# Low parts of the mixing stage's weights, made during the first feed forward and fetched from DRAM

## The chip, the core and the metric

The program runs on one core of a Trainium2 chip. The metric is the device time of one execution in microseconds (us). The core's engines each run their own instructions strictly in the program's order: TensorE (PE in the profile, PEld for its weight loads), VectorE (DVE), ScalarE (ACT), GpSimd (POOL) and SyncE (SP). SP, ACT and POOL also issue DMAs; an issue that has to wait holds up what stands behind it on that engine.

## What is computed

The reference is a chain of transformer blocks on 512 tokens of width 1024, all in float32: a dilated-window attention, a differential attention, and then a second block, cut here to what matters:

```python
x = x + 0.5 * swiglu_ffn(rms_norm(x, ffn1_norm[l]), ffn1_w_in[l], ffn1_w_out[l])   # first feed forward
h = rms_norm(x, mix_norm[l])
q_a, k_a, v_a, q_i, k_i, w_i, u_s, q_m, gates = jnp.split(h @ w_in[l], offsets, axis=-1)
o_a = indexed_sparse_attention(...) @ w_o_a[l]
y_s = jax.nn.gelu(s5_layer(u_s, ...))                 # a complex recurrence over the tokens
glu_a, glu_b = jnp.split(y_s @ w_glu[l], 2, axis=-1)
o_b = glu_a * jax.nn.sigmoid(glu_b)
o_m = memory_attention(q_m, m_k, m_v) @ w_o_m[l]
g = jax.nn.sigmoid(gates.reshape(b_, s_, N_BRANCHES, D_MODEL))
merged = g[:, :, 0] * o_a + g[:, :, 1] * o_b + g[:, :, 2] * o_m
x = x + merged @ w_out[l]                             # ends the mixing stage
x = x + 0.5 * swiglu_ffn(rms_norm(x, ffn2_norm[l]), ffn2_w_in[l], ffn2_w_out[l])
```

## The kernel before, in words

**Weights in two parts.** Each product of activations with weights is done as three matmuls in a rounded format (`mm3`, lines 153 to 155): every operand is kept as a high part and a low part, the low part being what the rounding leaves over. Activations are `uh`, `ul` (or `yh`, `yl`), weights `wh`, `wl`. Weights come in pieces of 128 partitions by 1024 columns (a few by 512 or 904). `_load` (line 300) issues a piece's DMA on SP into `raw`, of which there are two buffers. `_split` makes the two parts with `split`: ACT rounds `raw` into `wh` (line 175), DVE subtracts `wh` from `raw` into `wl` (line 176). `wh` and `wl` are rings of four buffers. A piece is split up to three pieces ahead of its use; PE needs about 5.4 us for a piece of the feed forward.

**Steps.** `tok` (tokens by output columns) and `feat` (columns by tokens) put their pieces in the list `plan` and add a step. Their sums stand in four PSUM banks, `pp`. In the first feed forward a step fills all four: PE can begin the next step only as ACT and DVE empty them (`sg`, lines 923 and 924, for the hidden units; `xa`, line 1656, for the output).

**Side work.** Coroutines (`co`) put other work between the matmuls. They wait on a clock that only the matmuls' estimated times advance; the framework then schedules what was recorded, keeps each engine's list in that order or near it, and adds the waits. `prepare` (line 1355) starts one at the beginning of the first feed forward: it normalizes the memory tokens, makes the tables of the recurrence on POOL (`s5_setup`, lines 1060 to 1069) and stores them to DRAM one by one (`s5tab<-s5cs`, line 1068), and makes the bias table (`bias_table`). The tables pass through two buffers of the pool `aux`, with the tags `memx0` and `memx1`; a tag has one buffer here.

**The mixing stage.** `mix` first projects keys, index and memory queries, then the recurrence's inputs `us` and the queries `q`, and then runs the branches: gates from `w_in`, outputs by `w_o_m` and `w_glu`. Between these matmuls stand the memory attention, the choice of keys (`score`, 16 rounds of maximum and replace), the recurrence (`s5wr`, `s5wi`) and the sparse attention. Their matmuls stand in PE's one list among those of the projections.

Of the kernel before, what the change touches and what calls it, by code (L numbers as in the profile page):

```python
# [9 lines left out]
F32 = mybir.dt.float32  # L10
FR = mybir.dt.float32r
# [8 lines left out]
P = 128  # L20
D = 1024
S = 512
# [3 lines left out]
BIG = 3.0e38  # L26
RAW, RING, AHEAD = 2, 4, 2
RQ = 2

S5GAP, SPGAP = 10.0, 2.5  # L30
KKS, KKG, HDG = 2, 8.0, 10.0
# [9 lines left out]
class Act:  # L41


    def __init__(self, n):
        self.z = [None] * n
        self.done = set()
# [19 lines left out]
class Net:  # L66
    def __init__(self, ctx, tc, consts):
        self.tc, self.nc = tc, tc.nc
        pool = lambda name, bufs, **kw: ctx.enter_context(tc.tile_pool(name=name, bufs=bufs, **kw))
        self.open = lambda c, name, bufs: c.enter_context(tc.tile_pool(name=name, bufs=bufs, reuse_waits="tile"))  # L70
        self.consts = consts
        self.cpool = pool("consts", 1)
        self.rings = {"u": pool("u", 2), "y": pool("y", 2)}
        self.wraw = pool("wraw", RAW)
        self.wsplit = pool("wsplit", RING)
        self.small = pool("small", 2)
        self.pp = pool("pp", 4, space=PSUM)
        self.pa = pool("pa", 4, space=PSUM)
        self.dram = pool("dram", 1, space=DRAM)
        self.flip = self.open_xn = 0  # L80
        self.spare_dve = False
        self.clock, self.seq, self.heap = 0.0, 0, []
        self.steps, self.plan = [], []
        self.raws, self.ready, self.live = [], {}, 0


    def at(self, delay, fn):
# [203 lines left out]
    def _load(self):  # L291
# [10 lines left out]
            o += m  # L302
        self.raws.append(raw)

    def _split(self):
        i = self.next_split
        raw = self.raws[i]
        n, nk = raw.shape[2], raw.shape[1]
        h, l = (self.wsplit.tile([P, 1024], FR, name="w" + x, tag="w" + x)[:, :nk * n]
                .rearrange("p (k c) -> p k c", k=nk) for x in "hl")  # L310
        self.split(raw, h, l)
        self.ready[i] = [(h[:, j, :], l[:, j, :]) for j in range(nk)]
        self.raws[i] = None
        self.next_split += 1
        self.live += 1
        self._load()
# [101 lines left out]
    def roped(self, x, w_in, c0, out, tmp, flags):  # L418

        nc = self.nc  # L420
        for j0 in range(0, 4, 2):
            def ev(c, ps, tok, j0=j0):
                sw = tmp().tile([P, S], F32, name="rq", tag="rq", bufs=RQ)
                for b in range(0, P, 32):
# [75 lines left out]
    def dilated(self, u, w_in, y, enter):  # L500
# [53 lines left out]
        def gate0(c, ps, _):  # L554
            sg = self.silu_gate2(v["tmp"], ps[c], "rq", RQ)
            self.need(lambda: state.get("comb0"))
            self.gated(state["f0", c], [z[:, c, :] for z in state["y0"]], y, c, sg)
# [192 lines left out]
    def differential(self, u, w_in, lams, subln, linit, y, enter):  # L750
# [53 lines left out]
        for hh in range(2):  # L804
            def ev_gate(c, ps, _, hh=hh):
                if (hh, c) in heads:
                    sg = self.silu_gate2(v["tmp"], ps[c], "rq", RQ)
                    self.gated(heads[hh, c], [z[:, c, :] for z in heads["y", hh]], y, 4 * hh + c, sg)
# [546 lines left out]
    def prepare(self, a, pre, aux):  # L1355

        nc = self.nc
        v = {}
        gc = v["gc"] = pre.tile([P, 4], F32, name="gc")
        for i, nm in enumerate(("a_q_gain", "a_k_gain", "m_q_gain", "m_k_gain")):  # L1360
            for h in range(2):
                nc.gpsimd.dma_start(gc[h * 64:h * 64 + 64, i:i + 1], a[nm].unsqueeze(1))
        v["mkT"] = pre.tile([P, 2, 256], F32, name="mkT")
        v["mv"] = pre.tile([P, 2, 256], F32, name="mv")
        v["mk"] = set()
        m = v["mem"] = Act(KT)
        m.g = [tuple(aux.tile([P, 4, 256], FR, name="mT%d%s" % (i, x)) for x in "hl") for i in range(2)]
        m.z = [(g[0][:, j, :], g[1][:, j, :]) for g in m.g for j in range(4)]
        self.mixv = v

        def gen():
            g = self.gain(aux, a["mem_norm"], "gmem")
            for t in range(2):
                xt = aux.tile([P, D], F32, name="memx%d" % t)
                nc.gpsimd.dma_start(xt, a["mem"][t * P:(t + 1) * P, :])
                yield 5.0
                self.norm_u(aux, xt, self.row_rstd(aux, xt), g, t, m)
                yield 10.0
            yield from self.s5_setup(a, pre, aux)
            yield 5.0  # L1380
            v["btab"] = self.bias_table(a["rel_bias"], a["onehot"], aux)

        self.co(gen())

    def mix(self, u, a, enter, merged):

        nc, tc = self.nc, self.tc
        V, G = nc.vector, nc.gpsimd
        w = a["w_in"]
# [32 lines left out]
        def raw(name):  # L1422
            self.need(bm.free)
            return v["at"].tile([P, S], F32, name=name, tag="bm", bufs=bm.n), bm.take()
# [30 lines left out]
        def ev_heads(key, nh, dst, col):  # L1455
            def ev(t, ps):
                def gen():
                    r, held = raw(key + "r")
                    yield from self.heads_T(r, room(), v["st"], ps, nh, v[dst], v["gc"][:, col:col + 1], t)
                    held[0] = True  # L1460
                    flags[key].add(t)
                self.run_now(gen())
            return ev
# [26 lines left out]
            self.co(gen())  # L1490

        self.tok(ux, [(w, 1220, 256)], ev_heads("qm", 4, "qmT", 2), by="t")
        self.feat(ux, [(w, 964, 256)], ev_us)
        self.add(start_s5)
        self.tok(ux, [(w, 0, 512)], ev_heads("q", 8, "qaT", 0), by="t")
# [2 lines left out]
        def branch(b, o, wo, first, last):  # L1498
            nk = len(o.z)
            if first:  # L1500
                for f in range(0, KT, 2):
                    def ev_first(c, ps, _, f=f):
                        nc.scalar.activation(v["M"][f + c], ps[c], AF.Tanh, scale=0.5)

                    self.feat(ux, [(w, 1476 + b * D + f * P, 256)], ev_first)
                for f in range(0, KT, 2):
                    def ev_prod(c, ps, _, f=f):
                        M = v["M"][f + c]
                        V.scalar_tensor_tensor(M, M, 1.0, ps[c], op0=OP.add, op1=OP.mult)

                    self.feat(lambda: o, [(wo, f * P, 256)], ev_prod, nk=nk)
                return
            for f in range(0, KT, 2):
                th = []

                def ev_gate(c, ps, _, th=th):
                    s = v["sg"].tile([P, S], F32, name="sgm", tag="sgm")
                    nc.scalar.activation(s, ps[c], AF.Tanh, scale=0.5)
                    th.append(s)

                def ev_o(c, ps, _, f=f, th=th):
                    M = v["M"][f + c]
                    V.scalar_tensor_tensor(th[c], th[c], 1.0, ps[c], op0=OP.add, op1=OP.mult)
                    G.tensor_tensor(M, M, th[c], op=OP.add)
                    if last and f == KT - 2:
                        self.at(1.5, lambda: finish(f + c))

                def ev_glu(c, ps, _, f=f, th=th):
                    if c < 2:
                        return  # L1530
                    M = v["M"][f + c - 2]
                    s = v["sg"].tile([P, S], F32, name="glt", tag="sgm")
                    nc.scalar.activation(s, ps[c], AF.Tanh, scale=0.5)
                    V.scalar_tensor_tensor(s, s, 1.0, ps[c - 2], op0=OP.add, op1=OP.mult)
                    V.scalar_tensor_tensor(s, th[c - 2], 1.0, s, op0=OP.add, op1=OP.mult)
                    V.scalar_tensor_tensor(M, s, 0.5, M, op0=OP.mult, op1=OP.add)

                self.feat(ux, [(w, 1476 + b * D + f * P, 256)], ev_gate)
                if last and f == KT - 2:
                    def most():  # L1540
                        for k in range(KT - 2):
                            self.at(1.2 * k, lambda k=k: finish(k))
                    self.add(most)
                if b == 1:
                    self.feat(lambda: o, [(wo, f * P, 256), (wo, D + f * P, 256)], ev_glu, nk=nk)
                else:
                    self.feat(lambda: o, [(wo, f * P, 256)], ev_o, nk=nk)
# [8 lines left out]
        merged.done = set(range(NT))  # L1556
        branch(2, om, a["w_o_m"], True, False)
        branch(1, ys, a["w_glu"], False, False)

        def leave():  # L1560
            self.need(lambda: v.get("a done") and v.get("s5 done"))
            v["inner"].close()
# [15 lines left out]
    def run(self, a, out):  # L1578
        nc, tc = self.nc, self.tc
# [4 lines left out]
        pool = lambda c, name, bufs=1: self.open(c, name, bufs)  # L1584
# [100 lines left out]

        def enter_mix():
            self.need(lambda: len(self.mixv["mk"]) == 2)
            s3.close()
            return s2

# [121 lines left out]
```

## Time and profile before

| | us |
|---|---|
| median of 3 runs (2160.23 to 2167.46) | 2166.17 |
| the profiled execution | 2165.69 |
| its span, first to last instruction | 2163.9 |
| outside the span | 1.8 |
| PE busy | 2103.0 (97%) |
| DVE busy | 1237.9 (57%) |

The steps here are sums on the profiled execution, which lies 0.5 us under the median. In the span the first feed forward runs from about 920 to 1305 us, the projections that open the mixing stage follow from 1330, and the stretch in which the attentions and the recurrence stand between the matmuls goes from 1390 to 1610. A row of the timeline gives the start, the time taken, engine, line, operation and tiles, and in brackets how long the engine had been idle before and what ended that.

### The profile page before, as it was taken

Reading aid. Unit: us, or ns where it says so; the run is one execution under the profiler, and the core shown is the slowest. Engines: PE = TensorE matmul, PEld = TensorE weight load, DVE = VectorE, ACT = ScalarE, POOL = GpSimd, SP = SyncE. Lnnn points to the kernel's source line nnn. Section 1 sums busy time; section 2 is a strip of 40 time slices with the busy share of each in tenths; the row PEclk is TensorE's granted clock in tenths of the full one; section 3 lists DMA queues with packets and bytes.
Section 4 is the critical chain, followed back from the end, with each engine's and each line's share of the span. In section 5 each row is a group of like instructions: output and inputs, shape, how many; then the busy total and the mean of one; then the engine's idle time right before and its main releaser. Section 6 shows DMA issues by size and latency. Waiting matters only on the chain.

```text
span 2163.9 us, 27643 instructions
## 1 busy us (share of the span) xinstructions
PE 2103.0 (97%) x10217; PEld 1709.3 (79%) x10217; DVE 1237.9 (57%) x2673; ACT 938.7 (43%) x1885; POOL 234.5 (11%) x322
## 2 busy tenths in 40 slices
PE   7999999999999999999999999988899999999998
PEld 6888988889888776788888888755567888888887
DVE  5645457454667677876543337889885454333334
ACT  4746455464545655555223234433344234223223
POOL 0000000000000000110970000124431100000000
PEclk9999999999999999999999999989999999999999
DMA  5222222212233212233343334222243323333332
GB/s 176 88 69 69 69 70 63 83 59 69 80 127 127 88 59 69 98 120 109 117 146 98 98 98 154 79 60 74 64 143 97 110 81 99 97 97 98 98 98 78
DMA packets 152055, 204.11 MB, mean 94 GB/s; under 512 B 9848, under 2 KB 111240, under 8 KB 151920
## 3 DMA queue, kind: packets, MB, share of 16 engines
q1 hardware_dynamic: 138368, 170.70, 25.8%
q10 hardware_dynamic: 8352, 15.14, 2.4%
q0 software_dynamic: 5200, 16.50, 2.1%
q8 instruction: 80, 1.31, 0.3%
q14 instruction: 55, 0.45, 0.1%
HBM read 191.80 MB, written 10.51 MB: 93 GB/s over the span
## 4 chain that ended last, share of the span: by engine, by line
PE 49%; DVE 8%; ACT 2%; DMA 1%; issue 1%; POOL 1%; ACTq 0%; DVEq 0%; POOLq 0%; SPq 0%
PE pp L153 15%; PE pp L154 15%; PE pp L155 15%; PE pa L159 3%; PE pa L164 1%; DVE wl L176 1%; DVE s5wi L1148 1%; DVE score L1262 1%; DVE s5wr L1147 1%; DMA raw<-in_w_in 1%; ACT wh L175 1%; DVE s5t L1150 0%; ACT p L438 0%; DVE m L1261 0%; POOL s5wr L1142 0%
## 5 line engine op out<-in xcount | busy, mean ns | idle before, releaser
L176 DVE TENSOR_TENSOR wl<-raw,wh 128x1024 fp32r<-128x1024 f32 (+1 forms) x320 | 410.4, 1283 | 496.1 <-ACT wh L175 494.9
L175 ACT CAST wh<-raw 128x1024 fp32r<-128x1024 f32 (+1 forms) x320 | 333.7, 1044 | 636.8 <-PE pp L154 287.5
L153 PE MATMUL pp<-uh,wh 128*128 128x512 f32 (+1 forms) x1232 | 485.0, 394 | 0.2 <-DVE sg L445 0.2
L154 PE MATMUL pp<-ul,wh 128*128 128x512 f32 (+1 forms) x1232 | 478.2, 388 | 1.0 <-DVE ul L282 1.0
L155 PE MATMUL pp<-uh,wl 128*128 128x512 f32 (+1 forms) x1232 | 477.5, 388 | 0.0
L153 PEld LDWEIGHTS pp<-uh,wh 128*128 128x128 f32 x1232 | 232.0, 189 | 54.4 <-issue 9.9
L155 PEld LDWEIGHTS pp<-uh,wl 128*128 128x128 f32 x1232 | 232.4, 189 | 46.0 <-issue 0.6
L154 PEld LDWEIGHTS pp<-ul,wh 128*128 128x128 f32 x1232 | 233.0, 189 | 43.7 <-DVE ul L282 1.2
L153 PE MATMUL pp<-wh,uh 128*128 128x512 f32 (+2 forms) x592 | 237.9, 403 | 0.3 <-ACT wh L175 0.2
L154 PE MATMUL pp<-wl,uh 128*128 128x512 f32 (+2 forms) x592 | 229.2, 388 | 0.5 <-DVE wl L176 0.4
L155 PE MATMUL pp<-wh,ul 128*128 128x512 f32 (+2 forms) x592 | 228.6, 387 | 0.0
L153 PE MATMUL pp<-yh,wh 128*128 128x512 f32 (+1 forms) x464 | 176.0, 379 | 0.0
L154 PE MATMUL pp<-yl,wh 128*128 128x512 f32 (+1 forms) x464 | 175.1, 377 | 0.0
L155 PE MATMUL pp<-yh,wl 128*128 128x512 f32 (+1 forms) x464 | 174.8, 377 | 0.0
L425 ACT COPY rq<-pp 32x512 f32<-32x512 f32 x256 | 148.0, 578 | 58.0 <-PE pp L155 52.8
L153 PEld LDWEIGHTS pp<-wh,uh 128*128 128x128 f32 x592 | 127.8, 216 | 21.2 <-issue 4.6
L154 PEld LDWEIGHTS pp<-wl,uh 128*128 128x128 f32 x592 | 128.3, 217 | 17.3 <-DVE wl L176 1.8
L155 PEld LDWEIGHTS pp<-wh,ul 128*128 128x128 f32 x592 | 127.6, 215 | 16.6 <-issue 0.3
L153 PE MATMUL pp<-wh,yh 128*128 128x512 f32 x304 | 119.2, 392 | 0.1
L154 PE MATMUL pp<-wl,yh 128*128 128x512 f32 x304 | 118.8, 391 | 0.0
L155 PE MATMUL pp<-wh,yl 128*128 128x512 f32 x304 | 118.6, 390 | 0.0
L438 ACT ACTIVATE sm<-sm,nm 128x128 f32<-128x128 f32 (+1 forms) x192 | 79.8, 417 | 54.4 <-DVE nm L437 54.1
(404 smaller groups left out, 2774.4 us busy)
## 6 DMA issues: line engine op xcount, KB each, us to landing
raw<-in_ffn_w_in SPq DMA_DIRECT2D x176, 256.0 KB, 3.1
raw<-in_dil_w_in SPq DMA_DIRECT2D x80, 512.0 KB, 3.6
raw<-in_ffn_w_out SPq DMA_DIRECT2D x44, 512.0 KB, 3.7
raw<-in_diff_w_in SPq DMA_DIRECT2D x32, 512.0 KB, 3.7
raw<-in_w_in SPq DMA_DIRECT2D x32, 512.0 KB, 3.7
raw<-in_dil_w_out SPq DMA_DIRECT2D x8, 512.0 KB, 3.7
raw<-in_diff_w_out SPq DMA_DIRECT2D x8, 512.0 KB, 3.6
s5tab<-s5cs POOLq DMA_DIRECT2D x8, 512.0 KB, 3.3
```

The lines of the kernel that those rows point to most:

```text
L153: mm(ps, a[0], b[0], start=first, stop=False)
L154: mm(ps, a[0], b[1], start=False, stop=False)
L155: mm(ps, a[1], b[0], start=False, stop=last)
L159: self.nc.tensor.matmul(ps, a, b, start=start, stop=stop)
L164: self.nc.tensor.transpose(ps, x, self.ident[:n, :n])
L175: self.nc.scalar.copy(h, src)
L176: return self.nc.vector.tensor_tensor(l, src, h.bitcast(F32), op=OP.subtract)
L425: nc.scalar.copy(sw[b:b + 32, :], ps[c][b ^ 32:(b ^ 32) + 32, :])
L438: nc.scalar.activation(sm, sm, AF.Exp, bias=nm, scale=-1.0, accum_out=den)
L1147: V.tensor_tensor_scan(wr, mag, wr, 0.0, op0=OP.mult, op1=OP.add)
L1148: V.tensor_tensor_scan(wi, mag, wi, 0.0, op0=OP.mult, op1=OP.add)
L1262: V.match_replace(sc[:, :n], m8, sc[:, :n], -BIG)
```

## The change

A new coroutine, `low_parts`, runs at the end of `prepare`'s side work, so in the second half of the first feed forward. `self.early` names the pieces of the mixing stage from `us` to the end of the second branch, 30 of them; the loop ends when the mixing stage opens (`early_on`), and gets 25 done. For each piece it loads the weights on POOL's queue into a buffer `wr0` (with the tag `memx0`), lets ACT round them into `wh0` (tag `memx1`), lets DVE subtract in place, and stores the result to DRAM as `low`, again on POOL's queue. Between these halves the coroutine waits 4 us of the estimated clock (`EGAP`). In the mixing stage a piece that has a stored low part is still loaded as before and rounded on ACT, but its `wl` is fetched from DRAM by a DMA on SP; the subtract on DVE is gone.

```diff
+    def low_parts(self, pool):
+        nc = self.nc
+        for i in range(*self.early):
+            yield EGAP
+            if not self.early_on:
+                return
+            parts, k0, nk = self.plan[i]
+            n = sum(p[2] for p in parts)
+            r, h = (pool.tile([P, 2, S], F32, name=nm, tag=tag).rearrange("p a b -> p (a b)")[:, :nk * n].rearrange(
+                "p (k c) -> p k c", k=nk) for nm, tag in (("wr0", "memx0"), ("wh0", "memx1")))
+            o = 0
+            for w, c0, m in parts:
+                nc.gpsimd.dma_start(r[:, :, o:o + m],
+                                    w[k0 * P:(k0 + nk) * P, c0:c0 + m].rearrange("(k p) c -> p k c", p=P))
+                o += m
+            yield EGAP
+            if not self.early_on:
+                return
+            self.split(r, h.bitcast(FR), r.bitcast(FR))
+            low = self.dram.tile([P, nk, n], F32, name="low")
+            nc.gpsimd.dma_start(low, r)
+            self.low[i] = low
...
-        self.split(raw, h, l)
+        if i in self.low:
+            self.nc.scalar.copy(h, raw)
+            self.nc.sync.dma_start(l.bitcast(F32), self.low.pop(i))
+        else:
+            self.split(raw, h, l)
...
             v["btab"] = self.bias_table(a["rel_bias"], a["onehot"], aux)
+            yield from self.low_parts(aux)
...
         def enter_mix():
             self.need(lambda: len(self.mixv["mk"]) == 2)
+            self.early_on = False
             s3.close()
             return s2
```

Line numbers after the change are larger by 2 at `split` and by 30 from the steps on. On DVE, in the first feed forward just behind the copies of the bias table (`brow`), the list was:

```order
L176 TENSOR_TENSOR wl<-raw,wh 128x1024 x3
L1656 SCALAR_TENSOR_TENSOR xa_7835<-pp,xa_7835 128x512
L1656 SCALAR_TENSOR_TENSOR xa_7836<-pp,xa_7836 128x512
L1656 SCALAR_TENSOR_TENSOR xa_7837<-pp,xa_7837 128x512
L1656 SCALAR_TENSOR_TENSOR xa_7838<-pp,xa_7838 128x512
L176 TENSOR_TENSOR wl<-raw,wh 128x1024 x4
L924 TENSOR_TENSOR sg<-sg,pp 128x512 x2
```

The same place on DVE after the change:

```order
L178 TENSOR_TENSOR wl<-raw,wh 128x1024 x2
L178 TENSOR_TENSOR wr_9418<-wr_9418,wh_9419 128x1024
L178 TENSOR_TENSOR wl<-raw,wh 128x1024
L1690 SCALAR_TENSOR_TENSOR xa_7835<-pp,xa_7835 128x512
L1690 SCALAR_TENSOR_TENSOR xa_7836<-pp,xa_7836 128x512
L1690 SCALAR_TENSOR_TENSOR xa_7837<-pp,xa_7837 128x512
L1690 SCALAR_TENSOR_TENSOR xa_7838<-pp,xa_7838 128x512
L178 TENSOR_TENSOR wr_9487<-wr_9487,wh_9488 128x1024
L178 TENSOR_TENSOR wl<-raw,wh 128x1024 x2
L178 TENSOR_TENSOR wr_9564<-wr_9564,wh_9565 128x1024
```

The first subtract of an early piece stands before the third `wl` and the four `xa`, which empty the `pp` banks; ACT's list has the matching rounding of `wr` at the same place, between two roundings of `raw`.

On POOL, the end of the tables of the recurrence was followed only by the stores of `xa` at the end of the feed forward:

```order
L1188 DMA btab<-brow 8x640
L1065 TENSOR_TENSOR s5cs<-e_8867,e_8868 128x512 x2
L1067 TENSOR_TENSOR s5cs<-s5cs,s5t 128x512 x2
L1068 DMA s5tab<-s5cs 128x1024
L1668 DMA x_82<-xa_7835 128x1024
```

After the change the early pieces stand there, a load and a store in turn:

```order
L1218 DMA btab<-brow 8x640
L1095 TENSOR_TENSOR s5cs<-e_8867,e_8868 128x512 x2
L1097 TENSOR_TENSOR s5cs<-s5cs,s5t 128x512 x2
L1098 DMA s5tab<-s5cs 128x1024
L320 DMA wr_9418<-in_w_in 128x4x256
L328 DMA low<-wr_9418 128x1024
L320 DMA wr_9487<-in_w_in 128x4x256
L328 DMA low<-wr_9487 128x1024
```

No load of an early piece moved ahead of the tables; each load of `wr` waits for the store before it, since they use one buffer.

On SP, the DMA list of the mixing stage's gates and `w_o_m` was:

```order
L300 DMA raw<-in_w_in 128x2x512 x4
L300 DMA raw<-in_w_in 128x4x256 x8
L300 DMA raw<-in_w_o_m 128x2x256 x4
L300 DMA raw<-in_w_in 128x4x256 x2
L300 DMA raw<-in_w_glu 128x2x256 x2
```

After the change, at the change from the gates to `w_o_m`:

```order
L302 DMA raw<-in_w_in 128x4x256
L339 DMA wl<-low 128x1024
L302 DMA raw<-in_w_o_m 128x2x256
L339 DMA wl<-low 128x1024
L302 DMA raw<-in_w_o_m 128x2x256
L339 DMA wl<-low 128x512
```

The fetch of a low part stands between the loads of `raw`, one for each piece.

## Rows read from the trace of the kernel before

**Rows 1.** Page, part 1: busy us (share of the span) and instructions.
```profile
PE 2103.0 (97%) x10217; PEld 1709.3 (79%) x10217; DVE 1237.9 (57%) x2673; ACT 938.7 (43%) x1885; POOL 234.5 (11%) x322
```

**Rows 2.** Stretches A:B: length, busy PE, PEld, DVE, ACT, POOL, PE clock, DMA.
```profile
1131.00:1300.00 169.00, 169.00 (x747) 139.96 (x746) 58.08 (x63) 46.09 (x55) 0.00 (x0) 1.00 0.32 97
1392.00:1608.00 216.00, 184.63 (x784) 123.09 (x784) 192.50 (x399) 79.37 (x195) 86.80 (x80) 0.94 0.28 80
1400.00:1420.00 20.00, 16.41 (x63) 10.82 (x62) 16.45 (x44) 6.66 (x17) 6.04 (x7) 0.83 0.08 27
```

**Rows 3.** Whom PE waited for, 1340 to 1680: us, times, longest.
```profile
PE pa L164 <- ACT msm L438: 11.6, 8, 2.2
...
PE pa L164 <- DVE anm L437: 4.3, 1, 4.3
...
PE pp L153 <- ACT wh L175: 0.2, 1, 0.2
```

**Rows 4.** Stretch 1360:1610, instructions on `wl` alone: PE, PEld, DVE.
```profile
1360.00:1610.00 250.00, 74.32 (x190) 37.02 (x190) 31.11 (x26) 0.95 0.30 86
```

**Rows 5.** Timeline of DVE: first and last subtract in the stretch with PE's idle time.
```profile
1435.16 1.22 DVE L176 TENSOR_TENSOR wl<-raw,wh 128x1024 fp32r<-128x1024 f32 x1
...
1606.31 1.21 DVE L176 TENSOR_TENSOR wl<-raw,wh 128x1024 fp32r<-128x1024 f32 x1
```

**Rows 6.** DMA issues by queue: KB each, median us from issue to landing.
```profile
raw<-in_w_in SPq DMA_DIRECT2D x32, 512.0 KB, 3.7
...
s5tab<-s5cs POOLq DMA_DIRECT2D x8, 512.0 KB, 3.3
...
x<-xa POOLq DMA_DIRECT2D x4, 512.0 KB, 3.1
...
xb<-x POOLq DMA_DIRECT2D x4, 512.0 KB, 4.7
...
memx<-in_mem POOLq DMA_DIRECT2D x2, 512.0 KB, 4.5
...
raw<-in_w_o_m SPq DMA_DIRECT2D x4, 256.0 KB, 2.6
```

**Rows 7.** What SP's queue waited for, 1340 to 1600: us, times, longest.
```profile
SPq L300 <- DVE wl L176: 141.2, 15, 20.3
```

**Rows 8.** Roundings and subtracts, 1131 to 1300: ns min, median, max.
```profile
L175 ACT CAST wh<-raw x31: 1045/1053/1055, 1133.3 to 1296.7; 128x1024 fp32r<-128x1024 f32 x31
L176 DVE TENSOR_TENSOR wl<-raw,wh x31: 1216/1226/1226, 1134.3 to 1297.8; 128x1024 fp32r<-128x1024 f32 x31
```

**Rows 9.** Timeline of DVE, 1084 to 1098.
```profile
1085.57 1.39 DVE L176 TENSOR_TENSOR wl<-raw,wh 128x1024 fp32r<-128x1024 f32 x1 [4.14 <-ACT wh L175]
1091.01 1.75 DVE L176 TENSOR_TENSOR wl<-raw,wh 128x1024 fp32r<-128x1024 f32 x1 [4.05 <-ACT wh L175]
1092.68 2.02 DVE L1656 SCALAR_TENSOR_TENSOR xa<-pp,xa 128x512 f32<-128x512 f32 x3
1095.37 0.69 DVE L1656 SCALAR_TENSOR_TENSOR xa<-pp,xa 128x512 f32<-128x512 f32 x1 [0.67 <-PE pp L155]
```

**Rows 10.** Timeline of ACT around the first and the last early piece's place.
```profile
1084.48 1.06 ACT L175 CAST wh<-raw 128x1024 fp32r<-128x1024 f32 x1 [4.38 <-PE pp L155]
...
1302.13 1.05 ACT L175 CAST wh<-raw 128x1024 fp32r<-128x1024 f32 x1 [4.39 <-PE pp L155]
1305.07 0.63 ACT L204 ACTIVATE junk<-xa 128x512 bf16<-128x512 f32 x1 [1.89 <-DVE xa L1656]
```

**Rows 11.** Timeline of POOL, 1107 to 1130.
```profile
1110.75 2.54 POOL L1067 TENSOR_TENSOR s5cs<-s5cs,s5t 128x512 f32<-128x512 f32 x2
...
1119.47 3.97 POOL L1067 TENSOR_TENSOR s5cs<-s5cs,s5t 128x512 f32<-128x512 f32 x2
1123.74 0.60 POOL L1068 DMA_DIRECT2D s5tab<-s5cs  x1 [0.30 <-POOL s5cs L1067]
```

**Rows 12.** Landing of the table stores (`s5tab`), shortest, median, longest.
```profile
DMA to landing us min/median/max: 2.9/3.4/4.7
```

More of the change, by code (lines that the diff above doesn't have):

```diff
@@ L28 @@
 RQ = 2
+EGAP = 4.0
 S5GAP, SPGAP = 10.0, 2.5
@@ L84, in __init__ @@
         self.raws, self.ready, self.live = [], {}, 0
+        self.low, self.early, self.early_on = {}, (0, 0), True
     def at(self, delay, fn):
@@ L1492, in mix @@
         self.tok(ux, [(w, 1220, 256)], ev_heads("qm", 4, "qmT", 2), by="t")
+        first = len(self.plan)
         self.feat(ux, [(w, 964, 256)], ev_us)
@@ L1558, in mix @@
         branch(1, ys, a["w_glu"], False, False)
+        self.early = (first, len(self.plan))
         def leave():
```

## The prediction

> **What bounds the kernel now.** I read the page's busy times first. PE is busy for 2103.0 us of 2163.9 [rows 1], so 61 us of idle time are all that any change of the order can win, apart from what PE loses at its lower clock. The stretches come next [rows 2]. In the second half of the first feed forward (1131 to 1300) PE is busy for all of 169.00 us at full clock, DVE for 58.08 and ACT for 46.09; POOL does nothing. There is room for more work on DVE and ACT, but none for a wait: whatever holds PE up there is paid in full. In the mixing stage (1392 to 1608) PE is busy for 184.63 of 216.00 us, so 31.4 are idle, DVE for 192.50 (89%), and the granted clock is 0.94; a part of it, 1400 to 1420, shows 0.83 (the mean of stretches at 2.4 and at 1.2 GHz). At 0.94 some 6% of 216, 13 us, went to the lower clock. The list of PE's waits [rows 3] says who holds PE up there: exponentials of the memory attention (11.6 us) and row maxima (4.3), which stand behind DVE's list. Weights hardly count (0.2). So in the mixing stage DVE's load is the price of a step, and the weights' subtracts are part of that load: 31.11 us for 26 of them [rows 4], the first of which, 1.2, does not belong to the 25.
>
> **What the change removes.** 25 subtracts, 31.1 - 1.2 = 30 us of DVE, of which the last 19, from 1435.16 to 1606.31, lie in the stretch with the idle time: 15 of 1.2 us and 4 of half the columns, about 22 us [rows 5]. If DVE alone set the pace there, 22 us would come back, and with them up to 13 of clock: 36 in all. If PE's and DVE's waits for each other set it, little would: DVE is idle itself for 23.5 of the 216 us, and from 1400 to 1420, before the first of the 19, PE is idle for 3.6 us without any subtract in the way [rows 2]. I take the half of 22 and 4 us of clock: **15 us back**, between 0 and 36.
>
> **What it adds in the mixing stage.** 25 fetches of `wl` on SP. A fetch of this size lands 3.7 us after its issue [rows 6], against 1.2 for the subtract, but a ring slot is refilled three pieces before its use (16 us at 5.4 us each), and SP loses a wait: it now waits 141.2 us for subtracts to give `raw` free [rows 7], and for these pieces will wait for ACT's rounding alone. I cost the fetches at nothing; their cover is the ring, and without it each would show what it takes beyond the subtract, 2.5 us, 62 in all.
>
> **What it adds in the feed forward.** 25 roundings of 1.05 us on ACT and 25 subtracts of 1.23 on DVE (4 of each half as long) [rows 8]: 24 and 28 us beside 123 and 111 us of idle time [rows 2], free as work. What is not free is the wait that each brings into two strictly ordered lists. The order after the change shows it in two places.
>
> First, **the start**. On DVE the first early subtract stands between the `wl` of 1085.57 and that of 1091.01, ahead of the four `xa`; on ACT the first early rounding stands behind the rounding of 1084.48 [rows 9, 10]. It needs the first `wr`, and this load stands on POOL behind the last table, whose store is issued at 1123.74 [rows 11]; it also needs the table's buffer. So ACT and DVE stand still from 1086 on, and with them the `xa`. PE runs until its four banks are full, at 1095.37 [rows 9], where DVE was ready for the fourth of them. When does the load land? POOL's last tables go a little faster when DVE is quiet: two additions take 2.54 us in one row and 3.97 in another [rows 11]; I take 3 us off for the whole, so the last store is issued at 1120.7. It lands 3.3 us later [rows 6], 1124.0; the load is issued 0.3 later and lands after 4.2 us: 1128.5. Then rounding 1.05, subtract 1.23, `wl` 1.23, first `xa` 0.69, and 0.15 between them: 1132.9. PE has stood still for 1132.9 - 1095.4 = **37.5 us**. (Bounds: 3 us less with the shortest store and a load of 3.7; 6 more with the tables at their old pace and a load of 4.7.)
>
> On the last tables there is a rule: the Trainium skill, "SBUF — State Buffer", "Who interferes with whom", says that a DVE instruction with two SBUF inputs contends with a GpSimd instruction that reads SBUF. The rows agree: subtracts beside the tables take 1.39 and 1.75 us [rows 9], alone 1.23 [rows 8]. Without that rule the start would be 3 us longer.
>
> Second, **the rounds**. There is one buffer for `wr`, so the early pieces go round in a chain: load, rounding, subtract, store, next load. No POOL load of weights is in the trace. The nearest rows: POOL's loads of the same size land in 4.5 and 4.7 us, always with others in flight, SP's load of the same weights in 3.7 [rows 6]; POOL's stores in 3.1 and 3.3, from 2.9 to 4.7 [rows 6, 12]. I take 4.2 for the load, nearer to a load that flies alone, and 3.3 for the store. With 1.05 + 1.23 and 0.4 for the hand-overs (0.3 of it ahead of a store [rows 11]) a round is **10.2 us**; with the shortest values 9.3, with loads of 4.7 and stores of 3.9 it is 11.3, with the longest 12.1. A round with 512 columns (`w_o_m`) is 3.2 shorter: 1.1 for each transfer [rows 6], 1.0 for half the work.
>
> The places for the rounds are given: the 25th early rounding stands behind the rounding of 1302.13, so 24 rounds have 217.65 us (1084.48 to 1302.13) [rows 10], 9.07 each. A chain of 20 x 10.2 + 4 x 7.0 = 232 us does not fit. Its last load lands at 1128.5 + 232 = 1360.5, its rounding ends at 1361.6, and what stands next on ACT, the sum of squares of the finished `xa` that opens the mixing stage, stood at 1305.07: **56.5 us late**. PE can't run ahead to hide it: at each step's end (every 22 us) its four banks need the same two lists. The start's 37.5 us are within the 56.5, not added to them. Each microsecond of a round moves this by 24; at 9.3 the chain fits, and the start decides, with some 5 us more where two early pieces stand one weight piece apart: about 42. At 11.3 it is 83.
>
> **The sum.** 2165.7 (the profiled execution) + 56.5 - 15 = 2207.2 us. The profiled execution lies 0.5 us under the median; that is within this measurement's own spread. A change under 0.3% can't be told from none here.
>
> **The rivals.**
>
> *The rounds fit.* If a round takes 9.1 us or less, only the start costs: 42 - 15 = 27, 2193 us. For it: stores as short as 2.9 are there [rows 12]. Against it: it needs loads of 3.7 and stores of 2.9 every time, beside SP's own loads. One rule speaks for it: the Trainium skill, "DMA: Bandwidth & Descriptors", "Anatomy of one DMA — SWDGE (gpsimd) path", gives a DMA of POOL's queue as 2.0 us and the bytes at 436 GB/s, an estimate of 3.2 us for 512 KB either way. By it a round would be 9.1 us and the time 2193. The rows agree for the stores and not for the loads [rows 6]. Chance 0.18.
>
> *The rounds are slower.* If SP's stream of feed-forward weights stretches POOL's transfers to a round of 12.1 us, the chain ends 102 us late: 2165.7 + 102 - 15 = 2253 us. For it: loads issued together land in 4.7 and more. Against it: the table stores ran beside the same stream and landed in 3.4 as a rule [rows 12]. Chance 0.10.
>
> *The mixing stage pays it back.* DVE is the pace-maker of the mixing stage, all 31.4 us of PE's idle time and the 13 of clock go: 44. That is not slower than before if the feed forward loses less than 44, so only together with rounds that fit: 2165.7 + 42 - 44 = 2164 us. Against it: the idle time of PE ahead of the first of the 19 subtracts, where there is nothing to remove, and DVE's own 23.5 us of idle time. Chance 0.06.
>
> *The fetches come late.* The change then doesn't do what it says: PE waits for `wl`. At 2.5 us each, 62 us, and no gain: 2165.7 + 56.5 + 62 = 2284 us. Against it: the ring's 16 us. Chance 0.03.
>
> **How the numbers follow.** The forecast, rounds between 9.3 and 11.5 us with a gain between 0 and 36, has 0.63. Low end of the range: the start alone, 42, with a gain of 32: 2176. High end: rounds of 11.3 us, 83, with a gain of 3: 2246. Outside are the slowest rounds, the late fetches, the full payback and corners, 2 in 10. Faster by over 0.3% (under 2159): half of the payback, 0.03. Within 0.3%: its other half and the lowest corners of the forecast and of the rounds that fit, 0.05. Slower: 0.92.
>
> **What the next profile would show.** PE idle for some 37 us from 1095 on, with ACT waiting for a load of `wr` and DVE for ACT; no rounding of `raw` between 1086 and 1130. On POOL the loads of `wr` 10.2 us apart in the full rounds, each issued right when the store before it has landed. The first sum of squares of `xa` at about 1362 instead of 1305. From there to the end of the mixing stage some 15 us less than before, with `wl<-low` landing in under 5 us and no wait of PE for `wl`. I am wrong if ACT does not stand still behind the first `wr`, if a round takes under 9.3 us, or if the mixing stage gives back more than 36 us.

## The result, and the profile after

The changed kernel takes 2247.11 us in the median (2244.74 to 2250.46), the kernel before 2164.73 on the same occasion (2160.23 to 2167.46): a ratio of 1.0384, 95% interval 1.036 to 1.0407, or 82 us more. I had forecast 2207 us, between 2176 and 2246. The direction was right, the size about half. In the two profiled executions the span goes from 2163.9 to 2244.6 us, 80.7 more, and it helps to cut it at one instruction, the first sum of squares of the finished `xa`, which opens the mixing stage. Before it stood at 1305.07 [rows 10]. After:

ACT's timeline at the end of the first feed forward; the columns are start, length, engine, line, operation, and in brackets the idle time ahead and what ended it.

```profile
1372.02 1.05 ACT L177 CAST wh<-wr 128x1024 fp32r<-128x1024 f32 x1 [5.91 <-DMA wr<-in_w_glu]
1372.98 2.00 ACT L177 CAST wh<-raw 128x1024 fp32r<-128x1024 f32 x2
1383.15 1.05 ACT L177 CAST wh<-wr 128x1024 fp32r<-128x1024 f32 x1 [8.17 <-DMA wr<-in_w_in]
1384.10 0.63 ACT L206 ACTIVATE junk<-xa 128x512 bf16<-128x512 f32 x1
```

ACT waits 8.17 us for the load of the last early piece, rounds it, and only then sums up an `xa`: 1384.10, which is 79.0 us late. From there to the end it takes 860.5 us, against 2163.9 - 1305.1 = 858.8 before. So **the feed forward costs 79 us and the mixing stage gives nothing back** (1.7 us more). My terms were 56.5 and 15.

**Where the 79 us are.** The list of PE's waits over the second half of the feed forward (time in all, how often, longest), and then two stretches with the columns of [rows 2]:

```profile
PE pp L155 <- DVE xa L1690: 41.7, 3, 34.5
PE pp L155 <- ACT sg L953: 18.5, 8, 8.0
```
```profile
1095.00:1125.00 30.00, 0.00 (x0) 0.00 (x0) 0.00 (x0) 0.86 (x1) 21.63 (x22) 0.55 0.21 79
1150.00:1165.00 15.00, 9.24 (x34) 7.17 (x33) 5.48 (x7) 3.63 (x5) 2.00 (x3) 0.77 0.53 171
```

60.2 us are waits of PE for bank evacuations, 34.5 of them in one piece at the start, where PE, DVE and ACT all stand still and POOL alone works on its tables. The rest shows in PE's busy time up to the first sum of squares, before and after:

```profile
1084.00:1305.00 221.00, 221.00 (x976) 183.00 (x976) 81.96 (x83) 58.88 (x69) 36.58 (x32) 1.00 0.35 108
1084.00:1384.00 300.00, 239.80 (x1003) 193.66 (x1002) 101.47 (x107) 77.88 (x94) 63.73 (x82) 0.90 0.48 160
```

PE is busy for 18.8 us more. Some 10 of them are the clock: in or after each of the five longest pauses the granted clock is down at 1.2 GHz for a while (0.55 and 0.77 are means over stretches at both levels), 61 us in all; PE is busy for 20.5 of these, and its matmuls there start 0.43 us apart instead of 0.23. Some 6 are the 27 matmuls that PE has done more by then: it goes on with the feed forward's last product while ACT stands still for the last early piece. PE pays for that later, when it waits for the normalized `xa`, a wait that was not there before:

```profile
PE pa L166 <- DVE xn L274: 5.4, 1, 5.4
```

**The start and the rounds**, on POOL's timeline; a load of `wr` is issued right when the store before it has landed:

```profile
1116.86 0.60 POOL L1098 DMA_DIRECT2D s5tab<-s5cs  x1 [0.30 <-POOL s5cs L1097]
1120.09 0.78 POOL L320 DMA_DIRECT2D wr<-in_w_in  x1 [2.63 <-DMA s5tab<-s5cs]
1126.73 0.54 POOL L328 DMA_DIRECT2D low<-wr  x1 [5.87 <-DVE wr L178]
1130.29 0.76 POOL L320 DMA_DIRECT2D wr<-in_w_in  x1 [3.02 <-DMA low<-wr]
1136.89 0.54 POOL L328 DMA_DIRECT2D low<-wr  x1 [5.83 <-DVE wr L178]
1140.46 0.72 POOL L320 DMA_DIRECT2D wr<-in_w_in  x1 [3.03 <-DMA low<-wr]
1148.56 0.56 POOL L328 DMA_DIRECT2D low<-wr  x1 [7.38 <-DVE wr L178]
1152.17 0.72 POOL L320 DMA_DIRECT2D wr<-in_w_in  x1 [3.04 <-DMA low<-wr]
```
```profile
low<-wr POOLq DMA_DIRECT2D x21, 512.0 KB, 3.2
wl<-low SPq DMA_DIRECT2D x21, 512.0 KB, 3.2
wr<-in_w_in POOLq DMA_DIRECT2D x20, 512.0 KB, 5.0
```

The chain is there as forecast. Its first two rounds take 10.20 and 10.17 us (1120.09, 1130.29, 1140.46), the third 11.71. The difference lies between a load's issue and its rounding, 4.0 us in the first two and 5.5 in the third, as ACT's first three early roundings show:

```profile
1124.14 1.04 ACT L177 CAST wh<-wr 128x1024 fp32r<-128x1024 f32 x1 [40.08 <-DMA wr<-in_w_in]
1134.28 1.05 ACT L177 CAST wh<-wr 128x1024 fp32r<-128x1024 f32 x1 [8.16 <-DMA wr<-in_w_in]
1145.96 1.05 ACT L177 CAST wh<-wr 128x1024 fp32r<-128x1024 f32 x1 [8.72 <-DMA wr<-in_w_in]
```

All 25 early roundings end an idle time of ACT, and each time it is the load that ends it. The 14 full rounds up to 1275.04 take 154.95 us, 11.07 each, the six from 1309.32 to 1378.08 take 68.76, 11.46 each, the four of half the columns between them 34.28, 8.57 each. The page's part on DMA issues (KB each, median us to landing) says it in one number: the loads land after 5.0 us, the stores after 3.2.

**The mixing stage**, in a stretch moved by the 79 us, to be read beside the second line of [rows 2]:

```profile
1471.00:1687.00 216.00, 187.61 (x783) 126.20 (x783) 173.55 (x366) 78.51 (x191) 84.77 (x80) 0.91 0.38 118
```

DVE has 19 us less to do (173.55 after 192.50), and PE is idle for 28.4 us after 31.4. But the clock is 0.91 after 0.94: 41 us of the stretch are at 1.2 GHz after 27, and PE is busy for 38 and 24 us of them, which takes some 7 us of its work. PE's own list is not the same either. Matched by the tiles that they write and read, at least 88 of its 783 matmuls here stand at another place than before. Whom PE waits for here, beside [rows 3]:

```profile
PE pa L166 <- ACT msm L468: 11.9, 6, 3.0
PE pa L161 <- ACT apt L172: 8.0, 5, 3.1
...
PE pa L166 <- DVE anm L467: 3.8, 1, 3.8
```

The exponentials (`msm`) and the row maxima (`anm`) hold PE up as before. No `wl` is in the list: the fetches are hidden, as I had costed them.

### The profile page after: what moved, and what is told of

It reads as the page before. It is cut to its first block, busy times and chain, and to the rows that moved or that the text cites. A ratio compares the mean times of both kernels' runs of the same rounds, so it can differ in the third digit from the quotient of the medians.

```text
span 2244.6 us, 27808 instructions
## 1 busy us (share of the span) xinstructions
PE 2120.4 (94%) x10217; PEld 1719.6 (77%) x10217; DVE 1229.6 (55%) x2673; ACT 958.1 (43%) x1910; POOL 260.8 (12%) x375
## 4 chain that ended last, share of the span: by engine, by line
PE 33%; issue 8%; DMA 7%; DVE 7%; POOL 5%; ACT 3%; ACTq 0%; POOLq 0%; DVEq 0%; SPq 0%
PE pp L155 10%; PE pp L156 10%; PE pp L157 10%; PE pa L161 3%; DMA low<-wr 3%; DMA wr<-in_w_in 2%; PE pa L166 1%; ACT wh L177 1%; DMA s5tab<-s5cs 1%; POOL s5cs L1097 1%; POOL s5cs L1095 1%; DVE s5wr L1177 1%; DVE s5wi L1178 1%; DVE wr L178 1%; DVE wl L178 1%
## 5 line engine op out<-in xcount | busy, mean ns | idle before, releaser
L178 DVE TENSOR_TENSOR wl<-raw,wh 128x1024 fp32r<-128x1024 f32 (+1 forms) x295 | 367.4, 1248 | 399.7 <-ACT wh L177 398.4
L155 PE MATMUL pp<-uh,wh 128*128 128x512 f32 (+1 forms) x1232 | 490.4, 399 | 52.3 <-DVE xa L1690 34.5
L177 ACT CAST wh<-raw 128x1024 fp32r<-128x1024 f32 (+1 forms) x295 | 308.4, 1048 | 493.4 <-PE pp L156 214.7
L157 PEld LDWEIGHTS pp<-wh,ul 128*128 128x128 f32 x592 | 127.4, 215 | 16.7 <-issue 0.5
L178 DVE TENSOR_TENSOR wr<-wr,wh 128x1024 fp32r<-128x1024 f32 (+1 forms) x25 | 28.5, 1140 | 183.8 <-ACT wh L177 183.8
```

The costliest lines, as they stand in the source:

```text
L155: mm(ps, a[0], b[0], start=first, stop=False)
L157: mm(ps, a[1], b[0], start=False, stop=last)
L177: self.nc.scalar.copy(h, src)
L178: return self.nc.vector.tensor_tensor(l, src, h.bitcast(F32), op=OP.subtract)
```

## The experiments

Each is told beside runs of the kernel before on the same chip.

**1. The mixing stage alone.** One buffer of zeros is stored to DRAM, and 25 pieces fetch from it.

```
-            self.split(r, h.bitcast(FR), r.bitcast(FR))
...
+        self.nc.gpsimd.memset(r, 0.0)
+        low = self.dram.tile([P, 1024], F32, name="low")
+        self.nc.gpsimd.dma_start(low, r)
+        for i in range(self.early[0], self.early[0] + 25):
+            self.low[i] = low[:, :nk * n]
```

> Leaves out the early low parts: one buffer of zeros is stored to DRAM once by POOL, and the 25 pieces fetch their low part from there, so the first feed forward is as before and the mixing stage has the changed work at no price. Theory A (the mixing stage gives back almost nothing, since PE's pauses there are set by chains of short instructions over PE, DVE and ACT, and shorter pauses are paid with clock): 2158 to 2167 us against 2164.7 before. Theory B (my prediction's 15 us are real, and in the changed kernel a late and slow start of the stage ate them): 2146 to 2153 us. Theory C (the fetches cost something of their own): over 2167 us.

Measured: 2167.15 us against 2166.43, ratio 1.0001 (0.9993 to 1.001). The feed forward ends as before, or 1.4 us earlier (first sum of squares at 1303.6). The stretch of the mixing stage, here not moved:

```profile
1392.00:1608.00 216.00, 187.53 (x782) 126.00 (x780) 172.62 (x364) 77.92 (x191) 84.85 (x80) 0.91 0.39 117
```

DVE 20 us less, PE idle for 28.5 us, clock 0.91: the line of the changed kernel again, without its late start, and with the same order of PE's matmuls. The lower clock is no accident of one trace: over all executions and the whole span its mean is 0.9904 here and 0.9925 in the kernel before, some 5 us of 2166. Theory B, that the 15 us were there and the late start ate them, is gone.

**2. Without the fetches.** As in 1, but the pieces of which the low part was fetched take the high part in its place.

```
-            self.nc.sync.dma_start(l.bitcast(F32), self.low.pop(i))
+            self.low.pop(i)
+            l = h
```

> As the kernel of the mixing stage alone, but the 25 pieces fetch nothing: PE reads the high part in the place of the low part, so that neither subtract nor fetch is there. Tells the relief of DVE from the price of the fetches. If the fetches are free: within 3 us of the kernel with the fetches. If they cost what the relief gives: 8 us or more below it. Theory A wants 2158 to 2167 us, theory B 2146 to 2153.

Measured: 2164.29 us, 0.9993 (0.9985 to 1.0002). Between 0 and 3 us under the kernel with fetches. So the fetches eat at most 3 us, and the relief without them gives no gain that can be told from none.

**3. The feed forward alone.** The low parts are made and stored, and not used.

```
-            self.low[i] = low
```

> Makes and stores the 25 early low parts as the change does, but the mixing stage ignores them and subtracts as before: the price in the feed forward alone. The first sum of squares of xa should come at 1384, 79 us late, as in the changed kernel. If the mixing stage then runs as before: 2164.7 + 79 = 2244 us, so the whole change is the price of the feed forward and the mixing stage gives nothing. If a late start of the stage costs 6 us by itself and the relief gives these 6 back: 2250 us. If the relief gives 15: about 2260.

Measured: 2250.26 us (2245.34 to 2253.16), 1.0385 (1.037 to 1.0399). The first sum of squares comes at 1390.8, some 7 us later than I expected (the same chain of rounds, 265 us long instead of 259; the two kernels are the same up to there, and executions of this one lie up to 8 us apart), and from there the kernel takes 860.5 us, exactly as long as the changed one, which has 25 subtracts fewer. PE's matmuls of the mixing stage stand here in the order of the kernel before, all 783 of them. The whole loss is made in the feed forward.

**4. Two buffers for `wr`.**

```
-for nm, tag in (("wr0", "memx0"), ("wh0", "memx1")))
+for nm, tag in (("wr0", ("memx0", "gmem")[i % 2]), ("wh0", "memx1")))
```

> The early pieces use two buffers for wr in turn, so that a load need not wait for the store before it. The order then puts the 25 early roundings into 21 places of weight pieces (114 us, 4.8 us each) in place of 40. Theory: the place is set by the schedule's model and not by the chip, so the lists run ahead of the transfers again: start stall unchanged at 34.5 us of PE, rounds of 5.6 to 6.5 us against places of 4.8, so the first sum of squares of xa comes 60 to 82 us late and the time is 2222 to 2246 us. Rival (one buffer is the whole cause of the late rounds): only the start is lost, 2200 to 2206 us.

Measured: 2242.72 us, 1.035 (1.0337 to 1.0363). PE's longest wait at the start is 38.6 us, where I expected 34.5, the roundings stand from 1127.2 to 1279.7, 24 rounds of 6.35 us, and the first sum of squares comes at 1381.3, 76 us late. A faster chain hardly helps, because the schedule now puts its roundings 4.8 us apart in ACT's list (24 rounds in 21 weight pieces) instead of 9.1. In both kernels the places are closer than the transfers allow on the chip (6.35 and 11 us), and each early piece that comes too late makes ACT and DVE stand still. That the schedule's own estimate of a transfer sets the places is what I read from this; experiments 5 and 6 set the places by hand.

**5 and 6. Roundings put at places where the data is there.** `split` keeps its rounding instruction in `self.cast`; the early one is issued behind the last of these recorded, the first of them later. One kernel has one buffer and 12 pieces, 13.4 us apart, the other two buffers and 18 pieces, 8 us apart (`LATE` is 55 and 60 us, `EGAP` 5.2 and 3.2).

```
+        yield LATE
-            self.split(r, h.bitcast(FR), r.bitcast(FR))
+            with self.tc.issue_after(self.cast):
+                self.split(r, h.bitcast(FR), r.bitcast(FR))
```

> One buffer as in the change, but each early rounding is tied in ACT's list behind the rounding of raw that was recorded last at its time, the first of them 55 us of the matmul clock later, and only 12 pieces are made. In the order they stand 2.5 weight pieces (13.4 us) apart, from the tenth piece after the place of the change on, where the tables are done. Theory (the price of the feed forward is the lists' places running ahead of the transfers, not the work itself): no start stall, first sum of squares of xa at 1303 to 1308 us, time 2161 to 2169 us. Rival (the extra transfers, roundings and subtracts themselves slow the feed forward, 12/25 of 82 us): 2200 us or more.

> As the kernel with one buffer and placed roundings, but with two buffers for wr in turn, the first place 60 us of the clock later and 18 pieces, 1.5 weight pieces (8 us) apart, against 6.35 us for a round with two buffers. Theory: the feed forward costs nothing (first sum of squares of xa at 1303 to 1308 us), the mixing stage gives nothing, 2161 to 2169 us. Rival (work and transfers cost by themselves, 18/25 of 82 us): 2215 us or more. If the mixing stage pays after all once the feed forward is free: under 2159.

Measured: 2171.14 us with one buffer, 1.0021 (1.0012 to 1.003), and 2168.23 with two, 1.0009 (1.0 to 1.0017). The two answers on ACT's first sum of squares, one buffer ahead:

```profile
1313.03 0.63 ACT L207 ACTIVATE junk<-xa 128x512 bf16<-128x512 f32 x1 [1.89 <-DVE xa L1693]
```
```profile
1305.94 0.63 ACT L207 ACTIVATE junk<-xa 128x512 bf16<-128x512 f32 x1 [1.89 <-DVE xa L1693]
```

With two buffers PE waits for nothing from 1084 to 1305, although 18 loads, roundings, subtracts and stores run beside it: [rows 10]'s 1305.07 becomes 1305.94. With one buffer some roundings still come too late, PE waits 4.3 us for `sg`, the first sum of squares comes 5 us after the band I gave, and the time ends 2 us above its band. So the 79 us are the price of the places in the lists, not of the work or its transfers. No run places all 25 pieces so: with one buffer their rounds, 258 us in the changed kernel, are longer than the 217.65 us that the places span [rows 10]. And 18 fetched low parts still give nothing: no version that makes low parts early beats the kernel before.

**7. The subtracts twice.** The other way round, with the feed forward as in 1 and no fetches: 30 us more for DVE in the mixing stage.

```
+            self.split(raw, h, l)
+            self.split2(raw, h, l)
```

> The feed forward as before; in the mixing stage each of the 25 pieces has its subtract twice on DVE and fetches nothing: 30 us more of DVE in place of 30 us less. Theory A (DVE's load is not what PE waits for there): 2162 to 2175 us. Rival (DVE is the pace-maker near its limit, so that a load added costs although a load removed gives nothing): 2180 to 2200 us.

Measured: 2172.88 us, 1.0029 (1.0017 to 1.0041): 6.5 us for 30 us of work. DVE is busy for 198.84 us of the stretch and PE idle for 34.5. A load added costs a fifth of itself; the time lies in the upper part of theory A's band.

**8. No splitting at all.** Both parts of the 25 pieces are fetched, so ACT is relieved too.

```
-            self.nc.scalar.copy(h, raw)
+            self.nc.sync.dma_start(h.bitcast(F32), self.low[i])
```

> Leaves out both roundings and subtracts of the 25 pieces: both parts are fetched from a buffer of zeros in DRAM (raw is still loaded and not read). Takes 26 us off ACT as well as 30 off DVE. Theory A2 (PE's pauses are the lengths of the chains themselves): 2160 to 2169 us. Rival A3 (the short copies and exponentials stand behind the roundings in ACT's list, and that is the pause): 2145 to 2157 us.

Measured: 2166.68 us, 1.0 (0.9991 to 1.0008).

```profile
1392.00:1608.00 216.00, 189.49 (x798) 127.92 (x796) 173.70 (x364) 62.84 (x172) 85.37 (x81) 0.91 0.50 159
```

ACT falls from 79.37 to 62.84 us, PE's idle time from 31.4 to 26.5, and the clock from 0.94 to 0.91. The 4.9 us of idle time that go come back as matmuls at the lower clock. The time lies in theory A2's band, and rival A3 is gone.

**9. Relief in another place.** In DVE's timeline of the kernel before, ahead of the longest wait for `msm` in 1400 to 1405, stands no subtract of a weight:

```profile
1399.26 2.30 DVE L1147 TENSOR_TENSOR_SCAN s5wr<-s5cols,s5wr 128x512 f32<-128x512 f32 x1 [0.82 <-POOL s5wr L1142]
1401.48 0.26 DVE L1223 TENSOR_TENSOR mo<-pa,mden 128x128 f32<-128x128 f32 x1
1401.66 2.34 DVE L1148 TENSOR_TENSOR_SCAN s5wi<-s5cols,s5wi 128x512 f32<-128x512 f32 x1
1403.93 0.39 DVE L437 CUSTOM_DVE_ANT_0 msm<-pa,cst 128x256 f32<-128x256 f32 x1
```

The row maximum `msm` has no idle time ahead of it: it follows two scans of the recurrence at once. Nor do the subtracts stand where PE waits in the rest of the stretch from 1392 to 1608: of PE's 22 waits over 0.3 us there, 30.7 us in all, a subtract runs on DVE during two, which are 1.6 us long together, and a scan during seven, 13.2 us. Experiment 9 leaves all 16 scans out.

```
-                V.tensor_tensor_scan(wr, mag, wr, 0.0, op0=OP.mult, op1=OP.add)
-                V.tensor_tensor_scan(wi, mag, wi, 0.0, op0=OP.mult, op1=OP.add)
```

> The kernel before, without the 16 scans of the recurrence (2.25 us each, 36 us of DVE), which are left out of what is computed; the weights' subtracts are all there. In the trace row maxima of the memory attention stand in DVE's list behind these scans while PE waits. Theory P (what paces the mixing stage is what stands in DVE's list right ahead of the row maxima that PE waits for, and the subtracts don't stand there): 2135 to 2156 us, PE's idle time from 1392 to 1608 down from 31 to under 24. Rival Q (PE's pauses are chains of short instructions, and no relief of DVE pays, wherever it is): 2160 to 2168 us.

Measured: 2156.58 us against 2165.45, 0.9959 (0.9947 to 0.9972), 0.6 us above theory P's band and 3.4 below rival Q's.

```profile
1392.00:1608.00 216.00, 191.43 (x843) 128.17 (x844) 166.74 (x386) 82.74 (x201) 80.35 (x82) 0.96 0.29 86
```
```profile
PE pa L159 <- ACT apt L170: 5.8, 4, 2.9
PE pa L164 <- ACT msm L438: 4.4, 3, 1.6
```

The waits for `msm` fall from 11.6 to 4.4 us, PE's idle time to 24.6 (theory P wanted under 24), and the clock rises to 0.96. So 36 us off DVE in this place give 8.9, 30 us off in the subtracts' places give none. One rival is left for both: the schedule orders PE's list anew for each kernel. At least 73 of the 783 matmuls stand elsewhere in experiment 9, 88 in 1 and 7, 176 in 2, 82 in 8. No two runs differ in the relief and keep this order, so what a new order costs or gives is not told from what the relief does.

**10. The scans later.** All work is there; `yield 4.0` stands ahead of the two scans of each round.

> The kernel before, all of it, with the two scans of each round of the recurrence recorded 4 us of the matmul clock later, so that other work of DVE may stand ahead of them. Theory P: the row maxima come earlier, 2150 to 2162 us, unless the recurrence's own matmuls now wait for the later scans. Rival Q: 2162 to 2172 us.

Measured: 2177.15 us, 1.0056 (1.004 to 1.0072): 12 us slower. The waits for `msm` go out of the list of PE's longest, and waits for `apt` take their place, 13.7 us in 7 pauses, with the clock at 0.89. Both bands are missed. Theory P's exception is not what happened, for `apt` belongs to the sparse attention and not to the recurrence. Here 240 matmuls stand elsewhere; why `apt` now comes late stays open.

**11. Half of SP's stream.** 39 weight pieces of the feed forward load half of their rows, and ACT and DVE split that half alone.

```
+        if self.early[0] - 47 <= i < self.early[0] - 8:
+            nk //= 2
```

> The changed kernel, but 39 weight pieces of the first feed forward (those loaded beside the early rounds) load and split only half of their rows; PE reads that half twice. So SP's stream beside the early pieces is halved, and nothing in the round itself. Theory (the rounds are 11.2 us rather than 10.2 because SP's loads share the DMA engines with them): load to rounding down from a median of 5.1 to under 4.6 us, full rounds of 10.3 to 10.7, the first sum of squares of xa 10 to 20 us earlier than 1384. Rival (a load of POOL's queue takes 5 us by itself once stores run between): rounds and time as in the changed kernel, within 4 us.

Measured: 2240.98 us in one execution, beside 2168.13. From 1140 to 1380:

```profile
low<-wr POOLq DMA_DIRECT2D x19, 512.0 KB, 3.5
wr<-in_w_in POOLq DMA_DIRECT2D x17, 512.0 KB, 4.4
```

The loads land 0.6 us earlier than in the changed kernel (5.0 in the same stretch, 5.3 in experiment 3), so SP's stream is part of their length. The stores take 0.3 longer, so a full round is 10.70 us on average in the first 14 and 10.86 in the last six, and the first sum of squares comes at 1379.1, 5 us earlier, half of the least that I had expected, and less than the 6.7 us by which the changed kernel and experiment 3 differ with the same feed forward. So the time does not confirm it. Why the stores became longer stays open.

## Why the prediction was right or wrong

**The start: right.** Forecast 37.5 us of PE's time, measured 34.5. The wait stands where I put it (first `xa`, behind the first early subtract), for the cause that I named (the load stands on POOL behind the last table). The last table's store is issued at 1116.86 where I had 1120.7 and the kernel before 1123.74 [rows 11]: additions of tables now take 2.47 us beside a silent DVE, so I had taken too little off. The Trainium skill, "SBUF — State Buffer", "Who interferes with whom", has DVE's operations with two SBUF inputs contend with GpSimd's reads; the trace agrees, and by more than I allowed for.

**The rounds: the mechanism right, the term mis-sized.** I wrote 10.2 us for a full round and 7.0 for a half one; they took 11.19 (223.7 / 20) and 8.57. That is 20 x 1.0 + 4 x 1.6 = 26 us more, the chain began 4.4 us earlier than I had it (first rounding 1124.14, not 1128.5), and 56.5 + 26 - 4.4 = 78 against 79.0 measured. The failed step is the load: I took 4.2 us as "nearer to a load that flies alone". In the mean of the full rounds the rounding starts 5.12 us after the load's issue, the store is issued 2.60 later and the next load 3.46 after that; the sum had 4.2, 2.6 and 3.4. The first load, with none of SP's beside it, took 4.05, and the second, beside the ends of two, 3.99. But the chain ties the early subtract to those of `raw`, whose ends let SP issue its next loads, so each of the other loads flies beside one to four of SP's, and of the 20 with all columns 16 take over 4.8. My own upper bound, loads of 4.7, was the nearer row, and I had the reason for it in the rival of slower rounds. The rival of the fitting rounds fell with it. The Trainium skill's page "DMA: Bandwidth & Descriptors", section "Anatomy of one DMA — SWDGE (gpsimd) path", gives such a transfer 3.2 us, an estimate by its formula; the stores met it (3.2) and the loads did not (5.0).

**The mixing stage: wrong.** I wrote that "the half of 22 and 4 us of clock" come back, 15 us, because DVE is busy for 89% there. The changed kernel, and experiments 1, 2 and 8, stayed within some 2 us of no gain. Two things failed. A busy engine's load is not the wait: the subtracts stand in DVE's list where PE hardly waits (they run during 1.6 of its 30.7 us of waits), and experiments 7 and 9 show what a load was worth by its place (a fifth of the subtracts added, a quarter of the scans removed, none of the subtracts removed), each with its own order of PE's list. And the idle time that did go, 3 to 5 us, was paid back by a lower granted clock, where I had counted the clock as a second gain. I had named the sign of this myself (PE idle before the first of the 19 subtracts) and let it halve the term, where it should have taken it away. Why shorter pauses in sum came with more time at 1.2 GHz is seen in the rows, not explained; PE's matmuls, and so its pauses, stand in another order than before.

**The fetches: right.** They cost little or nothing: 3.2 us to landing, no `wl` among PE's waits, and experiment 2 without them is at most 3 us faster.

**The sum.** 2207.2 was short by the rounds less the earlier start (22.5) and by the mixing stage (16.7), together 39 us. The error of the rounds alone lay inside my bounds, and that of the mixing stage at the end of its own, a gain of 0; the top of the range, 2246, took rounds of 11.3 us together with a gain of 3, and the kernel had rounds of 11.2 and no gain. The end should have combined the bad ends of both terms.

## What to carry to other kernels

Work that is put into the gaps of strictly ordered lists costs by its waits, not by its length: where a schedule places an instruction by its own idea of a transfer's time, tie it to the place in the list where the data is really there (18 pieces so placed, with two buffers, moved the feed forward's end by 1 us, 25 that were not, with one, by 79). Price a transfer by rows that fly beside the traffic that the change itself will trigger. And before relieving a busy engine, look at what stands right ahead of the instruction for which the others wait; if the work to be removed is not there, expect nothing.

## What the runs showed of the hardware

The clock made pauses dearer than their length: of the 79 us lost in the feed forward, 60.2 were the pauses and some 10 matmuls at 1.2 GHz in or after them. And a load of 512 KB on POOL's queue, 4.05 us from issue to rounding when it flew alone, took up to 6.8 beside SP's loads, while the stores of the same size kept a median of 3.2.
